# A hybrid attention block with expert lookup: the first weight unit ahead of the modulation, low-part matmuls last, transpositions and sums of the attention placed later

## The chip, the cores and the metric

The kernel runs on one core of a Trainium2 chip. The metric is device time in microseconds (us) of one execution; the median of three runs before the change is 993.6 us (992.26 to 994.26). A core has five engines that run their own instruction streams in order and wait for one another by semaphores: TensorE (PE in the profile; PEld is its weight load), VectorE (DVE), ScalarE (ACT), GpSimd (POOL) and SyncE (SP), which issues most of the DMAs.

## What is computed

The reference is one encoder layer for 256 tokens of width 1024, cut here to what the change touches:

```
mod = silu(c) @ ada_w + ada_b                 # shift1, scale1, gate1, shift2, scale2, gate2
h   = rmsnorm(x) * (1 + scale1) + shift1
q,k,v of two head groups = h @ w_in           # 8 heads each
o_A = 2-D neighbourhood attention             # learned relative bias
o_B = dilated sliding-window attention        # distance bias
x   = x + gate1 * (concat(rmsnorm(o_A), rmsnorm(o_B)) @ w_out)
h2  = rmsnorm(x) * (1 + scale2) + shift2
x   = x + gate2 * peer(h2)                    # top-16 of 128 keys, twice, then 16384 experts
out = rmsnorm(x)
```

## The kernel before

Every weight matrix comes in units of 128x1024 fp32 (0.5 MB). A unit is **split** (`split`, L89): ScalarE writes its rounded high part `hi` (L91), and `lo = raw - hi` is made by GpSimd for units of kind "b" and by VectorE for kind "c" (L93). Activations are split in the same way (`h1[0]`, `h1[1]` for the high and low part: tiles h1h, h1l). Each product is then three matmuls: high by high, weights' low part, activations' low part. The kinds of the first units stand in `KW`, `KV` and `KX`, the order in which they are loaded in `order`, and `SEQ` says how the first loads on SyncE's queue alternate between pairs of blocks of `ada_w` ("p", 1 MB) and weight units ("u").

**Modulation and projection.** `mod` is made on VectorE: `block_sum` (L208) multiplies a 128x1024 block of `ada_w` by silu(c) and sums it, one column of `mod` per pass; for a scale column a small `gain` follows (L211). For slice k = 0 to 7 of the width the first two columns (shift1, scale1) are summed, then `modulate` makes h1h (L274) and a copy t (L275) on ScalarE and `h1l = t - h1h` on VectorE (L276). In the loop over k (L513) `qk_slice` multiplies slice k by one weight unit into four PSUM banks `qkp` (8 columns of 128, three matmuls each, in `slices`, L367); after every second slice a `v_unit` and an `x_unit` follow. `LEADS[k]` says how many units ahead are split.

**Attention.** From L542 there are 12 steps: four `v_unit`, four `qk_unit`, four `wo_unit` (the output projection of group A). In step i, after the step's matmuls, `more_ada` sums further blocks of `ada_w` (`ADA[i]` pairs, two passes each), and then a pipeline over 8 pairs of heads goes on: d = 0 `att_scores` (scores sp on TensorE, bias and minimum mn on VectorE at L429, exponentials p on ScalarE), d = 1 `att_turn` (transpositions pTp), d = 2 `att_values` (op on TensorE, os on VectorE at L455), and after a group's last pair `att_norm` (squares scr, mean ms on ScalarE; power rs on GpSimd; scaling of os on ScalarE, L479); d = 3 `att_block` turns the normed output by transpositions (tp, L464) into `oT`, which `wo_unit` multiplies.

**Second norm and queries.** After the second output projection, `spread` makes the inverse root mean square of each token as a row over all partitions with one matmul (rps, L260) from a diagonal dg (VectorE, L258). Three query units are multiplied with the unnormed activation, then h2 is made from rps in eight pieces.

**The rest.** From about 186 us the kernel streams the units of `u` and `v` of the experts through TensorE, with the key selection on VectorE beside the first of them.

The framework moves independent instructions past one another when it writes each engine's queue, so the order on an engine is not that of the code; `tc.issue_after` holds an instruction behind another. The lines that the change names:

```python
SEQ = 'pupupuuuupuuppuuuuuppuuu'
LEADS = (1, 3, 2, 3, 2, 2, 3, 3)
KW = 'bbcbcbcb'
```

Of the kernel before, what the change touches and what calls it, by code (L numbers as in the profile page):

```python
# [45 lines left out]
SEQ = 'pupupuuuupuuppuuuuuppuuu'  # L46
# [3 lines left out]
LEADS = (1, 3, 2, 3, 2, 2, 3, 3)  # L50
# [4 lines left out]
KW = 'bbcbcbcb'  # L55
# [14 lines left out]
def body(tc, xT, cols, ada, w_in, e2, w_out, wq, sk, u, v, fg, const, dil, out):  # L70
    nc = tc.nc
    with ExitStack() as top:
# [92 lines left out]
        def rstd(m, pool):  # L165

            r = pool.tile([128, 2], F32, name="rs", bufs=2)
            rstd.ins = nc.gpsimd.tensor_tensor(r, m, half, op=OP.pow).ins
            return r
# [4 lines left out]
        with ExitStack() as pre:  # L174
# [88 lines left out]
            def mean_sq(ssq, n):  # L263
                m = PA.tile([128, 2], F32, name="ms", bufs=2)
                for T, c in enumerate(ssq):
                    nc.scalar.activation(m[:, T:T + 2 // len(ssq)], c, AF.Identity, scale=1.0 / n, bias=eps)
                return m
# [54 lines left out]
            m1 = mean_sq([ssq[:, 0:2]], D)  # L322
            with tc.issue_after(bank.ins):
                xp.append(bank(PP, "S"))
# [24 lines left out]
            def more_ada():  # L349
                if ada_left:  # L350
                    ada_unit(*ada_left.pop(0))
# [15 lines left out]
            def slices(k, ps, w):  # L367

                for c in range(w[0].shape[1] // 128):
                    o = ps[c // 2][:, c % 2 * S:(c % 2 + 1) * S]  # L370
                    for x, a in ((0, 0), (0, 1), (1, 0)):
                        nc.tensor.matmul(o, w[x][:, c * 128:(c + 1) * 128], h1[a][:, k, :], start=False,
                                         stop=k == 7 and c % 2 == 1 and x == 1)
                    yield
# [8 lines left out]
            def qk_slice(k, hl):  # L383

                for c, _ in enumerate(slices(k, qkp, hl)):
                    if c == CP[k]:
                        next_block(k + 2)
# [93 lines left out]
            def wo_unit(g, c2):  # L481
                hl = unit()
                hv = [t.rearrange("p (k c) -> p k c", k=4) for t in hl]
                for cc in range(2):
                    ps = PM.tile([128, 512], F32, tag="mm", name="ps")
                    for k in range(4):
                        mm3(ps[:, :S], hv[0][:, k, cc * 128:(cc + 1) * 128], hv[1][:, k, cc * 128:(cc + 1) * 128],
                            oT[0][:, 4 * g + k, :], oT[1][:, 4 * g + k, :], k == 0, k == 3)
                    b = 2 * c2 + cc
                    nc.vector.scalar_tensor_tensor(x_s[:, b, :], ps[:, :S], mod[:, 2, b:b + 1], x_s[:, b, :],  # L490
                                                   op0=OP.mult, op1=OP.add)
# [21 lines left out]
            for k in range(8):  # L513
                lead[0] = LEADS[k]
                with tc.issue_after(dg_ins):
                    hl = unit() if k < 7 else None
# [27 lines left out]
            steps += [lambda i=i: wo_unit(0, i) for i in range(4)]  # L544
            for i in range(len(steps)):
                if i == E2AT:
                    nc.sync.dma_start(e2s, e2.rearrange("p (h s k) -> p h s k", h=NH, s=6))
                steps[i]()
# [4 lines left out]
                for n in range(ADA[i]):  # L553
                    more_ada()
# [5 lines left out]
                for d in range(4):  # L560
# [13 lines left out]
                    if d == 3 and h == 6:  # L574
                        for b in range(4):
                            att_block(g, b)
# [30 lines left out]
            rps = spread(rstd(m, PA), PP, "S")  # L607
            rb2 = PA.tile([128, S], F32)
            nc.scalar.activation(rb2, rps, AF.Copy)
            early = []  # L610
            for i in range(NQ):
                hl = unit()
                ps = PM.tile([128, 512], F32, tag="mm", name="ps")
                mmT(ps[:, :S + 2], hl, xg)
# [410 lines left out]
```

## Time and profile before

| what | value |
|---|---|
| median of three runs | 993.6 us (992.26 to 994.26) |
| the profiled execution: its time | 992.28 us |
| its span, from first to last instruction | 990.5 us |
| mean granted TensorE clock | 0.985 |
| PE busy | 961.8 us (97%) |
| DVE busy | 721.0 us (73%) |
| ACT busy | 545.5 us (55%) |
| POOL busy | 446.3 us (45%) |

Around the span lie 1.8 us of the profiled execution's time. Busy shares are means over stages with different limits: the same engine can wait in one stage and set the pace in the next. A granted clock of 1.00 is TensorE's upper level (2.4 GHz), 0.50 its lower one (1.2 GHz), and a value between them is a stretch that has both.

### The profile page before, as it was taken

The numbers are of one execution on the slowest core, as the hardware profiler recorded it, in microseconds if no ns is written. First come the engines' busy times: TensorE is split into PE (matmuls) and PEld (weight loads), VectorE is DVE, ScalarE is ACT, GpSimd is POOL, SyncE is SP. The second block draws the span as 40 slices with busy tenths as digits, with TensorE's granted clock in tenths as the row PEclk, the third lists the DMA queues.
The fourth block names the chain that finished last, engine by engine and source line by source line (L and its number), as shares of the span: only waits on it lengthen the run. The fifth ranks groups of instructions, "written<-read, shape, count | busy, mean of one in ns | idle before, by whom it ended". The sixth has DMA issues, their size and how long they took to land.

```text
span 990.5 us, 17375 instructions
## 1 busy us (share of the span) xinstructions
PE 961.8 (97%) x6325; PEld 876.6 (89%) x6325; DVE 721.0 (73%) x1679; ACT 545.5 (55%) x1009; POOL 446.3 (45%) x200
## 2 busy tenths in 40 slices
PE   7899998999999999999999999999999999999996
PEld 4897887999999999999999999888888888888885
DVE  6958877799993677788888887677555555555555
ACT  3465666645444666666666565545555545445553
POOL 3677546677888677777777776000000000000002
PEclk8998999999999999999999999999999999999998
DMA  9777675355654455555554555688666566666672
GB/s 349 267 266 269 221 272 193 128 177 165 186 178 148 151 170 156 167 167 164 158 171 157 163 171 154 211 280 313 224 196 194 192 192 193 193 192 193 196 216 72
DMA packets 53397, 193.75 MB, mean 196 GB/s; under 512 B 5816, under 2 KB 6080, under 8 KB 53184
## 3 DMA queue, kind: packets, MB, share of 16 engines
q1 hardware_dynamic: 52672, 191.59, 59.3%
q8 instruction: 49, 0.80, 0.3%
q10 hardware_dynamic: 576, 1.05, 0.3%
q14 instruction: 36, 0.29, 0.1%
q0 software_dynamic: 64, 0.01, 0.0%
HBM read 190.52 MB, written 2.11 MB: 194 GB/s over the span
## 4 chain that ended last, share of the span: by engine, by line
PE 81%; DVE 1%; POOL 1%; ACT 1%; issue 1%; POOLq 0%; ACTq 0%
PE ps L130 14%; PE ps L131 14%; PE ps L132 14%; PE y L130 12%; PE y L131 12%; PE y L132 12%; PE gp L828 3%; PE scp L683 1%; DVE xgxd L586 0%; POOL GA L940 0%; DVE x_s L490 0%; POOL GA L946 0%; ACT xge2s L585 0%; ACT xsq L233 0%; PE tp L464 0%
## 5 line engine op out<-in xcount | busy, mean ns | idle before, releaser
L93 POOL TENSOR_TENSOR lo<-raw,hi 128x1024 fp32r<-128x1024 f32 x171 | 417.9, 2447 | 169.1 <-ACT hi L91 81.4
L91 ACT ACTIVATE hi<-raw 128x1024 fp32r<-128x1024 f32 x304 | 320.0, 1055 | 159.1 <-issue 61.7
L130 PE MATMUL ps<-h2h,hi 128*128 128x256 f32 x1128 | 320.5, 285 | 0.6 <-ACT GB L847 0.6
L131 PE MATMUL ps<-h2l,hi 128*128 128x256 f32 x1128 | 319.2, 283 | 0.0
L132 PE MATMUL ps<-h2h,lo 128*128 128x256 f32 x1128 | 319.0, 283 | 0.0
L93 DVE TENSOR_TENSOR lo<-raw,hi 128x1024 fp32r<-128x1024 f32 x133 | 163.3, 1228 | 135.5 <-issue 114.0
L130 PEld LDWEIGHTS ps<-h2h,hi 128*128 128x128 f32 x1128 | 216.3, 192 | 1.3 <-ACT GB L847 1.0
L131 PEld LDWEIGHTS ps<-h2l,hi 128*128 128x128 f32 x1128 | 216.5, 192 | 0.0
L132 PEld LDWEIGHTS ps<-h2h,lo 128*128 128x128 f32 x1128 | 216.3, 192 | 0.0
L130 PE MATMUL y<-hi,wx 128*128 128x512 f32 x512 | 199.3, 390 | 0.0
L132 PE MATMUL y<-hi,wx 128*128 128x512 f32 x512 | 199.3, 389 | 0.0
L131 PE MATMUL y<-lo,wx 128*128 128x512 f32 x512 | 199.3, 389 | 0.0
L896 POOL DMA_DIRECT2D g2d<-g2r x1 | 0.6, 594 | 317.0 <-ACT g2r L895 317.0
L814 DVE SCALAR_TENSOR_TENSOR gi<-iotaG,iT,gT 128x256 fp32r<-128x256 f32 x256 | 113.8, 476 | 31.5 <-PE gp L828 31.5
L130 PEld LDWEIGHTS y<-hi,wx 128*128 128x128 f32 x512 | 96.2, 188 | 20.2 <-ACT wx L866 0.2
L132 PEld LDWEIGHTS y<-hi,wx 128*128 128x128 f32 x512 | 96.1, 188 | 20.2 <-DVE wx L867 0.2
L131 PEld LDWEIGHTS y<-lo,wx 128*128 128x128 f32 x512 | 96.2, 188 | 19.5
L866 ACT ACTIVATE wx<-GB 128x256 fp32r<-128x256 f32 x90 | 37.7, 419 | 119.2 <-PE y L132 119.2
L831 DVE TENSOR_TENSOR gp<-gp,gl 128x512 f32<-128x512 f32 x64 | 44.6, 697 | 8.5 <-ACT gl L830 7.1
L811 DVE TENSOR_TENSOR jm<-iotaG,jT 128x512 fp32r<-128x512 f32 x64 | 43.6, 681 | 1.6 <-ACT iotaG L800 1.6
L208 DVE CUSTOM_DVE_ANT_0 araw<-araw,silb,col 128x1024 f32<-128x1024 f32 x24 | 41.9, 1759 | 1.1 <-DMA araw<-in_ada 1.1
L834 ACT ACTIVATE GB<-gp 128x368 f32<-128x368 f32 (+31 forms) x64 | 21.3, 332 | 37.6 <-DVE gp L831 37.6
(217 smaller groups left out, 1221.3 us busy)
## 6 DMA issues: line engine op xcount, KB each, us to landing
raw<-in_u SPq DMA_DIRECT2D x128, 512.0 KB, 3.6
raw<-in_v SPq DMA_DIRECT2D x128, 512.0 KB, 3.6
araw<-in_ada SPq DMA_DIRECT2D x20, 1024.0 KB, 7.6
raw<-in_w_in SPq DMA_DIRECT2D x24, 512.0 KB, 6.2
raw<-in_wq SPq DMA_DIRECT2D x16, 512.0 KB, 3.7
raw<-in_w_out SPq DMA_DIRECT2D x8, 512.0 KB, 8.0
GA<-in_ada SPq DMA_DIRECT2D x8, 512.0 KB, 5.2
e2s<-in_e SPq DMA_DIRECT2D x1, 1536.0 KB, 8.8
```

Source lines behind the costliest of these rows:

```text
L91: nc.scalar.activation(hi, raw, AF.Copy)
L93: ins = eng.tensor_tensor(lo, raw, hi.bitcast(F32), op=OP.subtract)
L130: nc.tensor.matmul(ps, wh, ah, start=first, stop=False)
L131: nc.tensor.matmul(ps, wh, al, start=False, stop=False)
L132: return nc.tensor.matmul(ps, wl, ah, start=False, stop=last)
L208: block_sum.ins = nc.vector.tensor_tensor_reduce(raw, raw, silb, 1.0, init, OP.mult, OP.add, m).ins
L811: nc.vector.tensor_tensor(jm, iotaG[:, None, :].to_broadcast([128, 4, 128]), jT[:, t0:t0 + 4, None].to_broadcast([128, 4, 128]), op=OP.is_ ...
L814: nc.vector.scalar_tensor_tensor(gi[:, t, :, :], iotaG[:, None, :].to_broadcast([128, 2, 128]), iT[:, t0 + t:t0 + t + 1], gT.bitcast(F32)[ ...
L828: nc.tensor.matmul(gp[:, t, :, :], jm[:, t, :], gi[:, t, :, :], start=True, stop=True)
L831: nc.vector.tensor_tensor(gp[:, :, 0, :], gp[:, :, 0, :], gl, op=OP.add)
L834: nc.scalar.activation(GB[:, m:, t0:t0 + 4], gv[:, done:, :], AF.Copy)
L866: nc.scalar.activation(wh, w, AF.Copy)
```

## The change

Four things are edited. (1) `SEQ` begins with a weight unit, so the first unit's DMA stands ahead of the first pair of `ada_w` blocks; its kind becomes "c" (VectorE makes its low part); its split is issued after the mean of squares, ahead of the diagonal; and `LEADS[0]` is 0, so that the second unit is no longer split in the same go. (2) `slices` multiplies both weight parts by h1h for all eight columns first and the weights' high part by h1l for all eight last. (3) In the attention `more_ada` stands behind the heads' pipeline of its step; group A's transpositions stand at the start of step 7 and group B's inside step 11, between the two halves of its `wo_unit`. (4) `spread` of the second norm is issued behind the first query unit.

```diff
-SEQ = 'pupupuuuupuuppuuuuuppuuu'
+SEQ = 'uppupuuuupuuppuuuuuppuuu'
-LEADS = (1, 3, 2, 3, 2, 2, 3, 3)
+LEADS = (0, 3, 2, 3, 2, 2, 3, 3)
-KW = 'bbcbcbcb'
+KW = 'cbcbcbcb'
...
             def slices(k, ps, w):
-                for c in range(w[0].shape[1] // 128):
-                    o = ps[c // 2][:, c % 2 * S:(c % 2 + 1) * S]
-                    for x, a in ((0, 0), (0, 1), (1, 0)):
-                        nc.tensor.matmul(o, w[x][:, c * 128:(c + 1) * 128], h1[a][:, k, :], start=False,
-                                         stop=k == 7 and c % 2 == 1 and x == 1)
-                    yield
+                for part in (((0, 0), (1, 0)), ((0, 1),)):
+                    for c in range(w[0].shape[1] // 128):
+                        o = ps[c // 2][:, c % 2 * S:(c % 2 + 1) * S]
+                        for x, a in part:
+                            nc.tensor.matmul(o, w[x][:, c * 128:(c + 1) * 128], h1[a][:, k, :], start=False,
+                                             stop=k == 7 and c % 2 == 1 and a == 1)
+                        if not part[0][1]:
+                            yield c
...
-            def wo_unit(g, c2):
+            def wo_unit(g, c2, between=None):
                 hl = unit()
                 hv = [t.rearrange("p (k c) -> p k c", k=4) for t in hl]
                 for cc in range(2):
+                    if cc and between:
+                        between()
...
-                with tc.issue_after(dg_ins):
+                with tc.issue_after(dg_ins if k else ms_ins):
                     hl = unit() if k < 7 else None
...
-            steps += [lambda i=i: wo_unit(0, i) for i in range(4)]
+            steps += [lambda i=i: wo_unit(0, i, att_blocks if i == 3 else None) for i in range(4)]
+
+            def att_blocks():
+                for b in range(4):
+                    att_block(1, b)
...
+                if i == 7:
+                    for b in range(4):
+                        att_block(0, b)
                 steps[i]()
...
-                for n in range(ADA[i]):
-                    more_ada()
...
-                for d in range(4):
+                for d in range(3):
...
-                    if d == 3 and h == 6:
-                        for b in range(4):
-                            att_block(g, b)
+                for n in range(ADA[i]):
+                    more_ada()
...
-            rps = spread(rstd(m, PA), PP, "S")
-            rb2 = PA.tile([128, S], F32)
-            nc.scalar.activation(rb2, rps, AF.Copy)
+            rs2 = rstd(m, PA)
...
-                mmT(ps[:, :S + 2], hl, xg)
+                ins = mmT(ps[:, :S + 2], hl, xg).ins
+                if i == 0:
+                    with tc.issue_after(ins):
+                        rps = spread(rs2, PP, "S")
+                    rb2 = PA.tile([128, S], F32)
+                    nc.scalar.activation(rb2, rps, AF.Copy)
```

How the edits move instructions is seen at three places. The first is VectorE's queue at the start of the program, before the change (sq is the square of x, araw a block of `ada_w`, xr the scaled x):

```order
L310 TENSOR_TENSOR sq_93<-sq_93 128x512
L208 ISA araw,mod<-araw,silb,col 128x1024
L208 ISA mod 128x1
L208 ISA araw,mod<-araw,silb 128x1024
L208 ISA mod 128x1
L211 TENSOR_SCALAR gain_107<-mod,gain_105,col 128x1
L338 TENSOR_TENSOR xr_170<-x_s,rps 128x256
L208 ISA araw,mod<-araw,silb,col 128x1024
L208 ISA mod 128x1
L276 TENSOR_TENSOR h1l<-t_186,h1h 128x256
```

The same place after it:

```order
L310 TENSOR_TENSOR sq_93<-sq_93 128x512
L93 TENSOR_TENSOR lo<-raw,hi 128x1024
L208 ISA araw,mod<-araw,silb,col 128x1024
L208 ISA mod 128x1
L208 ISA araw,mod<-araw,silb 128x1024
L208 ISA mod 128x1
L211 TENSOR_SCALAR gain_107<-mod,gain_105,col 128x1
L339 TENSOR_TENSOR xr_170<-x_s,rps 128x256
L208 ISA araw,mod<-araw,silb,col 128x1024
L208 ISA mod 128x1
L276 TENSOR_TENSOR h1l<-t_186,h1h 128x256
```

The first unit's low part now stands on VectorE, ahead of the first sums; the rest keeps its order.

The second is VectorE's queue in steps 1 and 2 of the attention, behind the four score passes (`st,mn<-sp`) of the first pair of heads, before the change:

```order
L208 ISA araw,mod<-araw,silb,col 128x1024
L208 ISA mod 128x1
L208 ISA araw,mod<-araw,silb,col 128x1024
L208 ISA mod 128x1
L429 ISA st,mn<-sp,e2s 128x256
L429 ISA mn 128x1
L429 ISA st,mn<-sp,e2s 128x256
L429 ISA mn 128x1
L208 ISA araw,mod<-araw,silb,col 128x1024
L208 ISA mod 128x1
L208 ISA araw,mod<-araw,silb,col 128x1024
L208 ISA mod 128x1
```

And after it:

```order
L208 ISA araw,mod<-araw,silb,col 128x1024
L208 ISA mod 128x1
L433 ISA st,mn<-sp,e2s 128x256
L433 ISA mn 128x1
L433 ISA st,mn<-sp,e2s 128x256
L433 ISA mn 128x1
L433 ISA st,mn<-sp,e2s 128x256
L433 ISA mn 128x1
L447 RECIPROCAL ri<-ri 128x2
L433 ISA st,mn<-sp,e2s 128x256
L433 ISA mn 128x1
```

Before, the second pair's last two score passes stood behind four sums; now all four stand behind one, and the other three sums follow them.

The third is ScalarE's queue at group A's norm, before the change (scr are the squares of the attention output os, ms their mean, q and pts parts of other heads):

```order
L476 ACTIVATE scr,osq<-os_901 128x512
L355 ACTIVATE q_174<-ps 128x256
L476 ACTIVATE scr,osq<-os_901 128x512
L91 ACTIVATE hi<-raw 128x1024
L266 ACTIVATE ms<-osq,eps 128x2
L597 ACTIVATE xge2s<-mod 128x8x2
L442 ACTIVATE pts<-pTp 128x512
L431 ACTIVATE p,ri<-st,mn 128x256
L479 ACTIVATE os_901<-os_901,rs 128x512 x2
```

And after it:

```order
L480 ACTIVATE scr,osq<-os_897 128x512
L356 ACTIVATE q_174<-ps 128x256
L480 ACTIVATE scr,osq<-os_897 128x512
L266 ACTIVATE ms<-osq,eps 128x2
L483 ACTIVATE os_897<-os_897,rs 128x512 x2
L91 ACTIVATE hi<-raw 128x1024
```

A unit's high part, which released a split on GpSimd ahead of the norm's power there, now stands behind the scaling of os; on GpSimd the power has moved ahead of one split.

## Rows read from the trace of the kernel before

**Rows 1.** Page: span; GB/s moved in 40 equal slices of the span.

```profile
span 990.5 us, 17375 instructions
GB/s 349 267 266 269 221 272 193 128 177 165 186 178 148 151 170 156 167 167 164 158 171 157 163 171 154 211 280 313 224 196 194 192 192 193 193 192 193 196 216 72
```

**Rows 2.** Windows: us; busy (x instructions) of PE, PEld, DVE, ACT, POOL; PEclk, DMA, GB/s.

```profile
79.91:119.44 39.53, 38.10 (x224) 30.76 (x224) 34.71 (x95) 22.54 (x59) 23.33 (x13) 0.87 0.64 232
...
119.44:151.78 32.34, 29.38 (x220) 26.76 (x219) 26.85 (x66) 19.65 (x50) 15.14 (x7) 0.95 0.70 269
...
89.66:99.66 10.00, 10.00 (x35) 8.39 (x34) 7.62 (x18) 4.44 (x11) 7.24 (x5) 0.50 0.85 310
...
130.20:133.50 3.30, 3.30 (x19) 3.30 (x18) 1.89 (x8) 3.01 (x10) 0.00 (x0) 0.54 0.60 211
...
250.00:300.00 50.00, 50.00 (x419) 50.00 (x418) 49.76 (x233) 22.99 (x36) 41.75 (x18) 1.00 0.59 181
...
186.00:975.00 789.00, 788.17 (x5223) 728.18 (x5222) 569.57 (x1394) 436.58 (x780) 328.80 (x138) 1.00 0.59 184
```

**Rows 3.** Waits of PE over the span: total us, times, longest us.

```profile
PE tp L464 <- ACT os L479: 4.5, 2, 2.3
PE qkp L372 <- DVE h1l L276: 3.9, 2, 3.7
PE qkp L372 <- ACT h1h L274: 3.1, 2, 2.8
PE sp L416 <- DVE mn L429: 1.3, 1, 1.3
...
PE rps L260 <- DVE dg L258: 0.9, 1, 0.9
```

**Rows 4.** Waits of DVE between 160 and 336 us, the longest.

```profile
DVE iT L762 <- PE rtp L756: 16.3, 1, 16.3
```

**Rows 5.** Timeline of DVE at the start: start us, us, instruction [idle before].

```profile
11.30 1.29 DVE L208 CUSTOM_DVE_ANT_0 araw<-araw,silb,col 128x1024 f32<-128x1024 f32 x1 [1.10 <-DMA araw<-in_ada]
...
13.77 0.27 DVE L211 TENSOR_SCALAR gain<-mod,gain,col 128x1 f32<-128x1 f32 x1
...
15.68 2.67 DVE L208 CUSTOM_DVE_ANT_0 araw<-araw,silb,col 128x1024 f32<-128x1024 f32 x1
...
18.28 2.55 DVE L276 TENSOR_TENSOR h1l<-t,h1h 128x256 fp32r<-128x256 f32 x1
...
22.01 0.27 DVE L211 TENSOR_SCALAR gain<-mod,gain,col 128x1 f32<-128x1 f32 x1
```

**Rows 6.** Timeline of ACT at the start.

```profile
11.53 0.26 ACT L266 ACTIVATE ms<-ssq,eps 128x2 f32<-128x2 f32 x1 [1.28 <-PE ssq L318]
13.19 0.69 ACT L256 ACTIVATE dg<-cst,rs 128x128 f32<-128x128 f32 x2 [1.40 <-POOL rs L168]
13.79 1.04 ACT L91 ACTIVATE hi<-raw 128x1024 fp32r<-128x1024 f32 x1
15.80 0.60 ACT L274 ACTIVATE h1h<-xr,mod,gain 128x256 fp32r<-128x256 f32 x1 [0.98 <-DVE xr L338]
```

**Rows 7.** Timeline of POOL: the splits of the start, and one in the attention.

```profile
14.91 2.36 POOL L93 TENSOR_TENSOR lo<-raw,hi 128x1024 fp32r<-128x1024 f32 x1 [1.04 <-ACT hi L91]
17.92 2.63 POOL L93 TENSOR_TENSOR lo<-raw,hi 128x1024 fp32r<-128x1024 f32 x1 [0.65 <-ACT hi L91]
...
126.14 2.37 POOL L93 TENSOR_TENSOR lo<-raw,hi 128x1024 fp32r<-128x1024 f32 x1 [5.07 <-ACT hi L91]
```

**Rows 8.** Timeline of ACT at group A's norm.

```profile
125.02 1.05 ACT L91 ACTIVATE hi<-raw 128x1024 fp32r<-128x1024 f32 x1
...
129.23 1.34 ACT L479 ACTIVATE os<-os,rs 128x512 f32<-128x512 f32 x2 [1.90 <-POOL rs L168]
```

**Rows 9.** Timeline of DVE in the attention, three rows.

```profile
119.36 2.80 DVE L208 CUSTOM_DVE_ANT_0 araw<-araw,silb,col 128x1024 f32<-128x1024 f32 x1
...
122.09 0.41 DVE L429 CUSTOM_DVE_ANT_0 st<-sp,dls 128x256 f32<-128x256 f32 x1
...
148.85 2.14 DVE L598 TENSOR_TENSOR xgxd<-mod,xge2s 128x16 fp32r<-128x16 f32 x1
```

More of the change, by code (lines that the diff above doesn't have):

```diff
@@ L265, in mean_sq @@
                 for T, c in enumerate(ssq):
-                    nc.scalar.activation(m[:, T:T + 2 // len(ssq)], c, AF.Identity, scale=1.0 / n, bias=eps)
+                    mean_sq.ins = nc.scalar.activation(m[:, T:T + 2 // len(ssq)], c, AF.Identity, scale=1.0 / n, bias=eps).ins
                 return m
@@ L322, in body @@
             m1 = mean_sq([ssq[:, 0:2]], D)
+            ms_ins = mean_sq.ins
             with tc.issue_after(bank.ins):
@@ L383, in qk_slice @@
             def qk_slice(k, hl):
-                for c, _ in enumerate(slices(k, qkp, hl)):
+                for c in slices(k, qkp, hl):
                     if c == CP[k]:
```

## The prediction

> **What bounds the kernel now.** I read the windows first, to find the stages in which TensorE waits. From 186 to 975 us it is busy 788.2 of 789.0 us at the full clock [rows 2]: there it is the bound, and the change leaves its work there as it is. So time can only be won or lost ahead of 186 us, and what is won there should pass through. One thing could stop it: VectorE's key selection beside the stream. But it waits 16.3 us for TensorE at its end [rows 4], so it has slack and does not hold the lead back.
>
> Then I read TensorE's waits [rows 3]. The reader is to see five: 3.7 us for the low part h1l of the first slice; 2.8 us for h1h of a later slice; 1.3 us for a score pass of VectorE; two of 2.2 to 2.3 us for the normed attention output os, one per group; 0.9 us for the diagonal of the second norm. Beside them stands the clock. After the wait of 1.3 us, among short matmuls and transpositions, TensorE ran 10.0 us at the lower level, and after the first wait for os 3.3 us at 0.54 on average [rows 2]. These cost 10.0 x 0.50 = 5.0 us and 3.3 x 0.46 = 1.5 us. All sums are made against the profiled execution's 992.3 us (its span of 990.5 us and 1.8 us around it), which lies 1.3 us under the median of 993.6; I subtract the gain from the median.
>
> **Term A, the start: gain 1.5 us.** The stall of 3.7 us has a cause in VectorE's rows: a sum that takes 1.29 us alone takes 2.67 us, and h1l, a quarter of its size, takes 2.55 us [rows 5]; at those times GpSimd made the low parts of the first two units, until 17.27 and 20.55 us [rows 7]. Both VectorE passes end 0.3 to 1.1 us after GpSimd's. So the two shut each other out. (The Trainium skill, page "SBUF — State Buffer", section "Who interferes with whom", says that a VectorE instruction with two inputs in SBUF and a GpSimd instruction that reads SBUF exclude each other, and that the one that starts first goes on undisturbed. The trace agrees with that here.)
>
> Now the first unit's high part can start behind the mean at 11.8 us and ends at 12.8 us (1.04 us), before the diagonal at 13.2 us needs ScalarE [rows 6]. Its low part takes VectorE about 1.2 us (as a sum alone, which is a pass of the same size), until 14.1 us. The first pair of sums, which ran from 11.30 to 14.04 us with its gain [rows 5], comes behind it: 14.1 + 2.7 = 16.8 us. That its block now lands half a MB later, 1.5 us at the 349 GB/s of the first slice [rows 1], is hidden: 12.8 us is before 14.1. Scaling x (0.4) and h1h (0.6) follow: the first real matmul starts at about 17.9 us instead of 16.4 us, 1.4 us later. Against that, 16 matmuls now need no low part: 16 x 0.12 = 1.9 us (50.0 us hold 419 of this size [rows 2]), until 19.8 us, while the next sum, alone, and h1l end at 17.2 + 1.3 + 0.4 = 18.9 us. The 3.7 us stall is gone. VectorE's next gain ends at 18.9 + 1.2 + 0.3 = 20.4 us where it ended at 22.28 us [rows 5], a lead of 1.9 us. But GpSimd's split of the second unit comes later (h1h and its copy go ahead of it on ScalarE): 19.4 to 22.0 us instead of 17.92 to 20.55 us [rows 7], and the next sum meets it. The chain of sums, splits and h1 that follows paces TensorE through the next slices, so its lead counts, not the stall: between 1.4 and 1.9 us, taken as 1.5. The bounds: -1.4 us if the chain is not faster and the first matmul is merely later, +3.7 us if the whole stall is won. The 2.8 us wait stays, since it is for h1h, not h1l. The new order of matmuls adds none.
>
> **Term B, the first pairs of heads: gain 3.6 us.** The score pass for which TensorE waited 1.3 us stood behind four sums; now it stands behind one. Without the wait the 10 us at the lower clock should not begin, so TensorE could win 1.3 + 5.0 = 6.3 us. VectorE allows less: from its first score pass at 79.91 us to group A's last os at 119.44 us it is busy 34.7 of 39.5 us [rows 2], 4.8 us idle, and in the new order one more sum (1.2 us) comes ahead of that os, as a count of the queue shows. 4.8 - 1.2 = 3.6 us. The bounds: 1.3 us if only the wait goes, 6.3 us.
>
> **Term C, group A's norm: gain 3.4 us.** From the score pass that ends at 122.5 us [rows 9], ScalarE, GpSimd and ScalarE again need until 130.6 us for os [rows 8], 8.1 us. In this a unit's high part (0.95 us until the next starts) stood ahead of the mean, and GpSimd's split of 2.37 us ahead of the power [rows 7]; both now stand behind. That takes up to 3.4 us from the chain, leaving 4.7. TensorE's own work between is 5.3 us before (122.5 to 127.8) and four matmuls less now, 4.8, so little or nothing of the 2.2 us is left; I count 1.9. With the wait the lower clock goes: 1.5 us. Bounds: 0 to 3.7 us. The postponed split is late for nobody: it belongs to a later step.
>
> **Term D, group B's norm: gain 2.2 us.** The second wait for os, 2.3 us, is covered from two sides: 12 matmuls (1.4 us) go ahead of the transpositions, and a small pass that sat 2.14 us on VectorE ahead of os [rows 9] now stands behind it. 1.4 + 2.1 exceeds 2.3; I leave 0.1. Bounds: 1.4 to 3.0 us, the upper one if a neighbouring wait for a PSUM bank goes too. For VectorE C and D need 5.6 us; its idle time there is 32.3 - 26.9 = 5.5 us [rows 2], so they fit, barely.
>
> **Term E, the second norm: gain 0.4 us.** Five more matmuls (0.6 us) go ahead of rps, out of a wait of 0.9 us. The h2 pieces start no earlier, as they hang on the diagonal, and TensorE meets them soon after; so 0.4. Bounds: 0 and 0.9 us.
>
> The sum is 1.5 + 3.6 + 3.4 + 2.2 + 0.4 = 11.1 us: 993.6 - 11.1 = **982.5 us**.
>
> **Rivals.**
> *VectorE paces the attention.* Terms B to D bring VectorE to its limit, and which passes meet a split of GpSimd is new. A meeting costs 1.4 to 1.5 us (2.67 or 2.80 against 1.29 [rows 5, 9]). Four more of them take 6 us from B to D: 988.5 us. For it: 34.7 busy of 39.5. Against: sums and splits are no more than before, and one split has left GpSimd. (By the skill's rule above, a meeting costs only the one that comes second; the time of this rival holds for meetings in which that is VectorE.)
>
> *The lower clock stays.* The waits shrink, but short matmuls and transpositions still stand in a row, TensorE falls to 0.50 where it did, and 5.0 and 1.5 us stay: at most the waits go, 1.5 + 1.3 + 1.9 + 2.2 + 0.4 = 7.3 us: 986.3 us. For it: the fall came after only 1.3 us of waiting. Against: the later attention steps, with the same short matmuls and no wait, ran at the full clock.
>
> *The lead is given back.* What is won by 150 us is lost before 186 us, where VectorE, ScalarE and GpSimd make the second norm: no change, 993 us. For it: the last sums now fall just there. Against: they are few (two passes, 2.4 us), and VectorE is idle there.
>
> *Slower: the lower clock through the attention.* If TensorE, now paced by VectorE in small waits between short matmuls, ran at the lower level for more than the 10 us that it does now, each 1 us of work costs 1 us more. Three steps of about 7 us, 21 us of work, at the lower level cost 21 us, less A, C, D and E (7.5 us, and B's 5.0 not won): 993.6 + 21 - 7.5 = 1007 us. It decides from 7.5 us of such work on. For it: the stretch at 89.66 us. Against: as above, later steps held the clock.
>
> **How the numbers follow.** The sum has 0.52 and, from 979.5 to 985.5 us, a range of its own; VectorE's pace 0.20; the lower clock that stays 0.12; given back 0.09; slower 0.07. The first three are faster by more than 0.2% (about 2 us, which is what a measurement of this kernel can tell): 0.84; given back is the same: 0.09; slower: 0.07. The range that holds 8 in 10 reaches from 978.5 us (A whole and B at 5 us instead of 3.6) up to 991.0 us, past VectorE's pace with two meetings more.
>
> **What would show it.** A: the wait for h1l gone, first matmul of slice 0 near 17.9 us, the gain of slice 1 near 20.4 us. B: no wait of sp for mn near 87 us, full clock from 86 to 100 us. C and D: waits of tp for os under 0.5 us each, full clock behind the first. E: wait for dg under 0.4 us. The stream begins 11 us earlier and lasts as long. It would be wrong if VectorE shows no idle time from 80 to 140 us and TensorE waits for score passes instead, if the clock row shows 0.50 in the attention for 10 us or more, or if TensorE's waits between 155 and 186 us grow by what was won.

## The result, and the profile after

The changed kernel takes 982.05 us (median of four runs, 981.32 to 984.14) beside 993.93 us for the kernel before in the same comparison (992.26 to 999.27): a ratio of 0.9875, with a 95% interval of 0.9834 to 0.9915. Its profiled execution took 981.43 us, with a span of 979.5 us, 11.0 us less than that of before [rows 1].

TensorE's waits ahead of the stream, in the changed kernel:

```profile
PE qkp L375 <- ACT h1h L274: 4.8, 3, 2.7
PE sp L420 <- DVE mn L433: 2.6, 2, 2.1
PE xp L245 <- DVE x_s L496: 1.6, 1, 1.6
PE tp L468 <- ACT pts L446: 1.3, 1, 1.3
...
PE tp L468 <- DVE oTl L472: 0.3, 1, 0.3
```

Against [rows 3], the waits for h1l, for os and for dg are gone. Those for h1h have grown, from 3.1 us in two waits to 4.8 in three, as the first matmul now comes later. New are 1.3 us at the first transposition, now for pts of another pair of heads, and a score pass that comes 2.1 us late.

The next views are windows. I cut the time ahead of the stream at four points that every kernel here has: the end of the projection's slices, the end of the fifth pair's output matmuls, the end of the eighth pair's, and the start of the query scores. First the kernel before, then the changed one, with the stream last. The counts show that the stages hold the same work: 306, 153 and 251 instructions on TensorE.

```profile
74.04:126.45 52.41, 50.98 (x306) 41.34 (x305) 46.76 (x115) 30.81 (x84) 31.14 (x17) 0.90 0.68 251
126.45:149.21 22.76, 20.56 (x153) 18.96 (x153) 17.34 (x45) 14.48 (x33) 11.45 (x6) 0.93 0.70 266
149.21:186.24 37.03, 31.40 (x251) 29.80 (x250) 26.71 (x46) 23.87 (x49) 25.25 (x15) 1.00 0.51 167
```

```profile
71.82:119.92 48.10, 45.51 (x306) 37.84 (x306) 46.49 (x114) 31.14 (x85) 34.55 (x17) 1.00 0.71 269
119.92:140.68 20.76, 18.64 (x153) 17.21 (x153) 16.74 (x45) 14.76 (x35) 10.61 (x5) 1.00 0.78 298
140.68:175.28 34.60, 31.47 (x251) 29.91 (x250) 27.39 (x48) 23.49 (x49) 26.35 (x15) 1.00 0.56 182
...
175.28:964.00 788.72, 787.79 (x5220) 727.55 (x5219) 568.53 (x1394) 436.40 (x780) 328.72 (x138) 1.00 0.59 185
```

The lead is 2.2 us at the end of the slices (74.04 to 71.82). The first five pairs add 4.3 us (52.41 to 48.10), the last three with group A's transpositions 2.0, the rest 2.4: together 10.9 us, which the stream keeps. These four numbers hang on one execution of the kernel before: against its second profile, below, they are 1.7, 6.6, 3.0 and 2.4 us. In the first stage the clock rose from 0.90 to 1.00, and VectorE is now busy 46.49 of 48.10 us.

VectorE at the start, and GpSimd's first splits:

```profile
12.68 1.22 DVE L93 TENSOR_TENSOR lo<-raw,hi 128x1024 fp32r<-128x1024 f32 x1 [2.38 <-ACT hi L91]
...
16.80 1.28 DVE L208 CUSTOM_DVE_ANT_0 araw<-araw,silb,col 128x1024 f32<-128x1024 f32 x1
...
18.05 0.42 DVE L276 TENSOR_TENSOR h1l<-t,h1h 128x256 fp32r<-128x256 f32 x1
...
19.66 0.27 DVE L211 TENSOR_SCALAR gain<-mod,gain,col 128x1 f32<-128x1 f32 x1
```

```profile
19.05 2.79 POOL L93 TENSOR_TENSOR lo<-raw,hi 128x1024 fp32r<-128x1024 f32 x1 [5.85 <-ACT hi L91]
```

The sum at 16.80 us and h1l meet no split and take 1.28 and 0.42 us, where they took 2.67 and 2.55 [rows 5].

### The profile page after: what moved, and what is told of

The parts are those of the page before. It is cut to its first block, busy times and chain, and to the rows that moved or that the text cites. A ratio compares the mean times of both kernels' runs of the same rounds, so it can differ in the third digit from the quotient of the medians.

```text
span 979.5 us, 17372 instructions
## 1 busy us (share of the span) xinstructions
PE 954.1 (97%) x6325; PEld 869.5 (89%) x6325; DVE 717.4 (73%) x1680; ACT 544.8 (56%) x1009; POOL 447.5 (46%) x199
## 4 chain that ended last, share of the span: by engine, by line
PE 82%; DVE 3%; issue 2%; POOL 1%; ACT 1%; DMA 0%; POOLq 0%; ACTq 0%; DVEq 0%
PE ps L130 14%; PE ps L131 14%; PE ps L132 14%; PE y L130 12%; PE y L132 12%; PE y L131 12%; PE gp L842 3%; DVE araw L208 1%; PE scp L697 1%; POOL lo L93 1%; PE op L457 1%; DMA raw<-in_u 0%; DVE x_s L496 0%; ACT hi L91 0%; DVE xgxd L597 0%
## 5 line engine op out<-in xcount | busy, mean ns | idle before, releaser
L130 PEld LDWEIGHTS y<-hi,wx 128*128 128x128 f32 x512 | 96.1, 188 | 20.1 <-ACT wx L880 0.2
```

The source lines that it names most:

```text
L130: nc.tensor.matmul(ps, wh, ah, start=first, stop=False)
```

## The experiments

Each experiment was timed 6 to 12 times beside the kernel before, before_again once. The changed kernel's row repeats the result above, and the time in the first row is the median beside it (the profiled execution took 992.28 us). The table gives the median, the ratio to before with its interval, the end of the slices, and the length of the three stages, all read from each run's trace at the four points named above.

| run | us | ratio (95%) | slices end | stage 1 | stage 2 | stage 3 |
|---|---|---|---|---|---|---|
| before, first profile | 993.9 | 1 | 74.0 | 52.4 | 22.8 | 37.0 |
| before, second profile | 994.9 | | 73.5 | 54.7 | 23.8 | 37.0 |
| start_unit | 993.2 | 0.9992 (0.9976 to 1.0008) | 71.7 | 50.8 | 23.8 | 38.4 |
| start_order | 988.0 | 0.9942 (0.9921 to 0.9963) | 73.6 | 47.9 | 20.5 | 40.3 |
| start_both | 986.0 | 0.9922 (0.9892 to 0.9951) | 71.5 | 47.9 | 20.0 | 40.2 |
| att_sums | 995.3 | 1.0015 (0.9997 to 1.0033) | 73.8 | 54.4 | 23.8 | 37.0 |
| all_but_order | 992.7 | 0.9982 (0.9966 to 0.9998) | 71.6 | 54.4 | 23.7 | 36.6 |
| all_but_unit | 984.0 | 0.9899 (0.9873 to 0.9924) | 73.8 | 48.8 | 20.1 | 34.6 |
| unit_on_gpsimd | 983.4 | 0.9892 (0.9868 to 0.9916) | 72.5 | 48.8 | 20.1 | 34.6 |
| the changed kernel | 982.1 | 0.9875 (0.9834 to 0.9915) | 71.8 | 48.1 | 20.8 | 34.6 |
| hold_before | 997.6 | 1.0027 (1.0015 to 1.0039) | 73.5 | 47.2 | 27.8 | 43.2 |
| hold_all_but_order | 994.2 | 0.9993 (0.9979 to 1.0008) | 72.0 | 47.3 | 27.8 | 42.8 |
| hold_all | 992.0 | 0.9972 (0.9958 to 0.9986) | 71.8 | 46.5 | 24.7 | 42.5 |
| hold_norm | 985.9 | 0.9914 (0.9891 to 0.9937) | 72.1 | 46.5 | 18.5 | 42.5 |

### The start's edits, together and apart

start_both is the kernel before with part (1) and part (2) of the change; start_unit has part (1) alone, start_order part (2) alone:

```diff
-                    for x, a in ((0, 0), (0, 1), (1, 0)):
+                for part in (((0, 0), (1, 0)), ((0, 1),)):
```

> The kernel before with the two edits of the start alone (the first unit's load, kind and split; the order of the matmuls in the slices). My theory (VectorE's chain of sums at the start sets the pace, and it has come free of the meetings with GpSimd): first matmul of slice 0 near 17.6 us, wait for h1l gone, projection's last slice 2.2 us earlier than before (near 71.8 us), and the whole lead kept: 2.2 us, about 991.5 us beside a before of 993.7. Rival (the attention of the kernel before, full of sums, takes the lead back): the slices end 2.2 us earlier, but the score wait in step 2 grows by as much and the time stays within 1 us of before.

> The kernel before with the edit of the first unit alone; the slices keep their order of matmuls. Theory (the chain of sums counts, not the order of the matmuls): h1l ends near 18.5 us, TensorE stalls for it only 0.5 to 0.9 us right behind its first matmul, slice 3 still starts near 38.0 us, and the lead at the end of the slices is 2.0 to 2.2 us. Rival (the reordered matmuls hide what is left of the stall): a stall of 1 us or more for h1l, and a lead of 1 us or less.

> The kernel before with the order of the matmuls in the slices alone. Theory: 16 matmuls (1.9 us) go ahead of the stall, so the wait for h1l shrinks from 3.7 to about 2.0 us, but the gain of slice 1 still ends near 22.3 us and the wait for h1h of slice 3 stays or grows: slice 3 starts at 40.1 us as before and the time stays within 0.5 us of before. Rival (the stall itself costs the time): slice 3 starts 1.5 to 1.9 us earlier, and so does all behind it.

At the end of the slices all three came out as the theory has it: part (1) brings 2 us there, part (2) nothing (73.6 and 71.5 us beside 73.5 to 74.0 and 71.7). But the order of the matmuls alone, which was to change nothing, made the kernel 5.8 us faster (0.58% of 994.7, by the ratio), all of it behind the slices: stage 1 fell from 52.4 or 54.7 to 47.9 us, stage 2 by 2 to 3 us. Neither theory nor rival had this. The matmuls are the same; what moved is where the framework puts instructions in the attention, on several engines. VectorE's second pair of score passes still stands behind four sums in this run. But TensorE has other work ahead of the score matmuls that wait for it. Its timeline in the kernel before, then in start_order:

```profile
86.95 0.44 PE L440 MATMUL pTp<-cst,p 128*128 128x128 f32 x2
88.72 1.35 PE L416 MATMUL sp<-k,q 64*128 64x256 f32 x6 [1.33 <-DVE mn L429]
```

```profile
86.57 0.66 PE L442 MATMUL pTp<-cst,p 128*128 128x128 f32 x4
87.06 1.00 PE L455 MATMUL op<-v,pts 128*128 128x64 f32 x8
88.31 1.13 PE L418 MATMUL sp<-k,q 64*128 64x256 f32 x6 [0.24 <-DVE mn L431]
...
94.90 1.82 PE L418 MATMUL sp<-k,q 64*128 64x256 f32 x8 [1.22 <-DVE mn L431]
```

Before, two transposition instructions stood there ahead of a wait of 1.3 us; here four of them and the first head's output matmuls (op) fill it, and 0.2 us is left. A wait of 1.2 us comes one step later, and the clock holds through the stage:

```profile
73.57:121.43 47.86, 45.81 (x306) 37.51 (x306) 44.28 (x114) 31.20 (x85) 33.88 (x17) 1.00 0.77 283
```

Stage 3 gives 3.2 us of it back (40.3 beside 37.0), half of it to a new stretch at the lower clock.

At group A's norm, too, the order alone puts the power ahead of the split. GpSimd, then ScalarE:

```profile
119.09 1.53 POOL L168 TENSOR_TENSOR rs<-ms,half 128x2 f32<-128x2 f32 x1 [5.61 <-ACT ms L266]
120.60 2.35 POOL L93 TENSOR_TENSOR lo<-raw,hi 128x1024 fp32r<-128x1024 f32 x1
```

```profile
120.66 1.34 ACT L481 ACTIVATE os<-os,rs 128x512 f32<-128x512 f32 x2 [0.69 <-POOL rs L168]
```

ScalarE stands idle for 0.7 us ahead of the scaling of os, where it stood 1.9 us before [rows 8].

### The sums alone

att_sums is the kernel before with `more_ada` behind the heads' pipeline, the first half of part (3):

```diff
-                for n in range(ADA[i]):
-                    more_ada()
                 if i < NH // 2:
...
                             att_block(g, b)
+                for n in range(ADA[i]):
+                    more_ada()
```

> The kernel before with the sums placed behind the heads' pipeline of their step, and nothing else; group B's transpositions stay where they were. Theory: the 1.3 us wait in step 2 goes and with it the 10 us at the lower clock (lead 6.8 us behind step 3's v_unit), VectorE then takes 2 to 2.5 us back in waits of the scores, group A's norm gives 2 us and keeps the clock, and group B's wait for os falls by the small pass that no longer stands ahead of it, from 2.3 us to about 0.3: in all 7.5 to 8.5 us, about 985.8 us. Rival (the clock stays down without the lead of the start, or falls elsewhere): a stretch of 10 us at 0.50 remains somewhere between 80 and 140 us, gain 3 us or less. Second rival (group B's part comes from the place of the transpositions): the wait for os stays at 2.3 us and the gain is about 5.7 us.

Gain: none. The ratio is 1.0015; this is the run in which the prediction's account of B and C fell. VectorE in this run, then its windows:

```profile
94.77 2.96 DVE L208 CUSTOM_DVE_ANT_0 araw<-araw,silb,col 128x1024 f32<-128x1024 f32 x1
...
97.66 1.73 DVE L556 TENSOR_TENSOR e2s<-cst,e2s 128x768 f32<-128x768 f32 x1
99.32 0.41 DVE L429 CUSTOM_DVE_ANT_0 st<-sp,e2s 128x256 f32<-128x256 f32 x1
```

```profile
98.50:109.50 11.00, 9.71 (x44) 8.88 (x45) 7.54 (x24) 4.71 (x13) 4.16 (x3) 0.53 0.56 197
```

Of the second pair only the last score pass still stands behind three sums (the first three behind two), and TensorE waits 0.5 us there. But two more sums and a mask of the bias (e2s) stand ahead of the third pair's last score pass. TensorE waits 3.6 us for it instead of 1.3, and the clock is down for the 10 us behind it as before, only later, as the first rival had it. At group A's norm nothing changed places either:

```profile
127.97 2.38 POOL L93 TENSOR_TENSOR lo<-raw,hi 128x1024 fp32r<-128x1024 f32 x1 [6.67 <-ACT hi L91]
130.31 1.71 POOL L168 TENSOR_TENSOR rs<-ms,half 128x2 f32<-128x2 f32 x1
```

A split still stands ahead of the power, and the wait for os is 3.2 us. Group B's wait for os stays at 2.3 us, the second rival's sign.

### Before again, and one part left out

before_again is the kernel before, profiled a second time; all_but_order and all_but_unit are the changed kernel without part (2) and without part (1); unit_on_gpsimd is the changed kernel with

```diff
-KW = 'cbcbcbcb'
+KW = 'bbcbcbcb'
```

> The kernel before, unchanged, profiled a second time: are its stretches at the lower clock a property of its order of work? Five stretches stood in the first profile (21.0, 41.5, 89.5 to 100, 130.0, and one near 11 us), 11.9 us of TensorE's work lost in all. Theory (the waits and the short matmuls of the order bring them): the same five places within 2 us, the one near 90 us again about 10 us long, span 989 to 992 us. Rival (they fall differently from execution to execution): other places or lengths, the loss differs by 3.4 us or more, and the span follows it.

> The changed kernel without the order of the matmuls in the slices (first unit, sums, transpositions and spread as changed). Theory (with the sums placed later the attention comes out in a good order only together with the slices' new order, since that alone changes what stands where in the queues): VectorE's queue in the attention is that of the sums' edit alone, the long wait of a score pass near 95 us (3.6 us there) comes again with its stretch at the lower clock, and of the lead only the start's 1.5 to 2.2 us and about 2 us of transpositions and spread stand against the 2.8 us lost: between 992 and 994 us. Rival (the edits add up: what the order brings alone, 4 to 6.5 us, is all that is missing): 986 to 988.5 us.

> The changed kernel without the edit of the first unit (its load, kind, split and the lead). VectorE's queue in the attention is that of the changed kernel. Theory (the first unit brings the start's lead of 2.2 us and nothing in the attention): no wait of 2.5 us or more for the scores, last projection matmul near 73.6 us, and 984 to 985.5 us. Rival (it also decides the attention, or the lead of the start is lost in it): within 0.8 us of the changed kernel's 982.

> The changed kernel with the first unit's low part on GpSimd instead of VectorE. Theory (a sum of VectorE and a split of GpSimd shut each other out): the split stands at 12.8 to 15.2 us, the first sum meets it and takes 2.5 to 2.8 us instead of 1.3, which is about what VectorE saves by not making the low part (1.2 us); first matmul within 0.5 us of 17.6 us, time within 1 us of the changed kernel. Rival (no exclusion, the low part is merely one pass less on VectorE): the sums take 1.3 us, first matmul near 16.3 us, and the projection ends 1.2 us earlier than in the changed kernel.

In the second profile of before the stretches fall elsewhere, as the rival has it. Its windows are

```profile
88.00:92.00 4.00, 3.84 (x17) 3.03 (x18) 3.99 (x10) 0.88 (x4) 4.00 (x3) 0.57 1.02 416
...
108.50:116.00 7.50, 7.50 (x37) 7.08 (x36) 4.90 (x20) 4.92 (x14) 3.31 (x2) 0.54 0.82 297
```

Where the first profile had 10 us in one piece from 89.66 us [rows 2], this one has 4 us there and 7 us twenty later. The stage lost as much to the clock, about 5 us (4.00 x 0.43 + 7.50 x 0.46), but no longer behind the one wait of 1.3 us. The rest of the rival did not come: the span does not follow the loss to the clock, it is 2.6 us longer at a slightly higher mean clock (0.988 beside 0.985). What grew are TensorE's waits in the attention, for score passes from 1.3 to 2.9 us, for os from 4.5 to 5.5 [rows 3]. The first of them:

```profile
PE sp L416 <- DVE mn L429: 2.9, 3, 1.4
```

all_but_order came out as the theory has it, at 992.7 us: VectorE's queue is that of att_sums, the wait of 3.6 us at the third pair is there again, and stages 1 and 2 are those of before. So is the wait for os at group B's norm, 2.3 us (5.5 less 3.2), although group B's transpositions stand where the change puts them:

```profile
PE tp L465 <- ACT os L480: 5.5, 2, 3.2
```

The edits don't add up: with part (2) the rest is worth 4 us on top of start_both, without it next to nothing beyond the start. all_but_unit, 984.0 us, shows part (1) worth about the start's 2 us and nothing in the attention. It has a stretch at 0.57 that the changed kernel lacks, yet its stage 1 is only 0.7 us longer, as it is in unit_on_gpsimd, which has such a stretch too. Most of the 1.7 us lost there (4.00 x 0.43) cost nothing, with VectorE busy throughout the stretch:

```profile
103.50:107.50 4.00, 3.96 (x18) 3.13 (x19) 4.00 (x14) 3.25 (x7) 1.59 (x1) 0.57 0.59 192
```

With the first unit on GpSimd, VectorE and GpSimd meet:

```profile
13.52 3.36 DVE L208 CUSTOM_DVE_ANT_0 araw<-araw,silb 128x1024 f32<-128x1024 f32 x1
```

```profile
13.26 2.54 POOL L93 TENSOR_TENSOR lo<-raw,hi 128x1024 fp32r<-128x1024 f32 x1
```

The split began first, took its usual time and ended at 15.80 us; the sum ended 1.1 us later, after 3.36 us instead of 1.22. That is 2.1 us lost for 1.2 saved; the slices end 0.7 us later than in the changed kernel and the first matmul comes 0.6 us later. The theory holds, at a price above the one expected (3.4 us against 2.5 to 2.8), and the first matmul and the time, 1.3 us above the changed kernel's, just miss what was forecast of them. (By the Trainium skill, page "SBUF — State Buffer", section "Who interferes with whom", the one that starts first goes on and the other blocks until it has ended. The two rows agree.)

### The sums held by hand

If VectorE's queue is what decides, the four score passes of a pair should stay together. For hold_before I expected by this that the wait of 3.6 us goes, that at most one stretch at the lower clock is left between 80 and 145 us, and 985.5 to 988 us. hold_before is att_sums with each step's sums held behind the last score pass of the step; hold_all_but_order and hold_all have the same hold in all_but_order and in the changed kernel:

```diff
                 for n in range(ADA[i]):
-                    more_ada()
+                    with tc.issue_after(att_scores.ins):
+                        more_ada()
```

> The kernel before with the sums behind the heads' pipeline, as in the run of the sums alone, and each step's sums now held in VectorE's queue behind that step's last score pass. All four score passes of a pair then stand together, and the queue of the attention no longer depends on the order of the matmuls in the slices. [...] Rival (the slices' order acts by itself, on TensorE): no better than the sums alone, 993 to 996 us.

> The changed kernel without the order of the matmuls in the slices, and with the sums held behind the score passes. Its queues in the attention are those of the next run. Theory: with the queue fixed by hand the slices' order is worth nothing more than what it hides at the start (0 to 1 us): within 1.5 us of the next run and 8 us or more ahead of the run without the hold (992.6). Rival (the order of the matmuls is itself what counts): 990 us or more.

> The changed kernel with the sums held behind the score passes. Theory (the 2.1 us wait of the scores near 101 us comes from two sums that stand between a pair's score passes and meet a split): that wait falls under 0.5 us and 1 to 2 us are won, 980 to 981.5 us. Rival (VectorE is busy throughout from 80 to 120 us, so the wait only moves, to the output passes os or to group A's norm): 981.5 to 984 us, the same as the changed kernel.

For stage 1 the theory holds, in all three: 46.5 to 47.3 us, also without any edit of the start, with waits for score passes of 0.6 us or less in all and no stretch at the lower clock. The hold also moves work, though: 12 of the sums fall into stage 1 instead of 16, so part of this may be the sums that have left it. And the times I had expected were missed by 9 to 12 us: stages 2 and 3 lost more than stage 1 won, hold_before and hold_all_but_order came out at their rivals' times or above, and hold_before, at 1.0027, is slower than before. TensorE's waits in hold_all, and GpSimd at its group A's norm:

```profile
PE tp L467 <- ACT pts L445: 2.6, 1, 2.6
PE tp L467 <- ACT os L482: 1.8, 1, 1.8
```

```profile
116.75 2.59 POOL L93 TENSOR_TENSOR lo<-raw,hi 128x1024 fp32r<-128x1024 f32 x1 [1.93 <-ACT hi L91]
119.31 0.72 POOL L168 TENSOR_TENSOR rs<-ms,half 128x2 f32<-128x2 f32 x1
```

The hold moved a split ahead of the power again, at both norms, and ScalarE stood 3.2 us at the scaling of os with the next pair's exponentials and pts behind it. The 2.6 us wait for pts is that. Behind it the clock fell for 7 us:

```profile
125.50:132.50 7.00, 7.00 (x26) 4.32 (x25) 2.75 (x10) 2.95 (x6) 2.35 (x1) 0.51 0.86 294
```

hold_all is 2.2 us faster than hold_all_but_order, more than the 1.5 us expected, and stage 2 has the difference (24.7 beside 27.8). In both a sum of VectorE stands ahead of three score passes shortly before group A's norm, and GpSimd starts two splits beside it. First hold_all_but_order, then hold_all:

```profile
109.43 3.45 DVE L208 CUSTOM_DVE_ANT_0 araw<-araw,silb,col 128x1024 f32<-128x1024 f32 x1
...
109.43 5.70 POOL L93 TENSOR_TENSOR lo<-raw,hi 128x1024 fp32r<-128x1024 f32 x2 [1.02 <-ACT hi L91]
```

```profile
108.94 1.27 DVE L208 CUSTOM_DVE_ANT_0 araw<-araw,silb,col 128x1024 f32<-128x1024 f32 x1
...
109.22 5.60 POOL L93 TENSOR_TENSOR lo<-raw,hi 128x1024 fp32r<-128x1024 f32 x2 [1.30 <-ACT hi L91]
```

In the one the sum starts with the split and takes 3.45 us; the score passes behind it and the norm's mean come 2.7 us later than in hold_all, TensorE waits 4.1 us for pts, and the clock is down for 10 us instead of 7. In the other the sum starts 0.3 us ahead of the split and takes 1.27 us. hold_before has the meeting of the first (3.38 us) and its wait of 4.1. This is read from three traces; no run varies the meeting alone.

### The norm's chain freed

If the held sums lost their time at the norms, because a high part stands ahead of the mean and one split more ahead of the power, then with these held back the waits of 2.6 and 1.8 us should fall under 1.3 and 0.5 us. By this I expected most of the time at the lower clock behind them to go, and 981 to 986 us. hold_norm is hold_all with one unit's split at each norm held behind the mean on ScalarE and behind the power on GpSimd (i counts the units):

```diff
+                with ExitStack() as held:
+                    for ins in behind if i in (25, 29) else ():
+                        held.enter_context(tc.issue_after(ins))
-                ready.append(split(i, loaded.pop(0) if loaded else load(i), eng))
+                    ready.append(split(i, loaded.pop(0) if loaded else load(i), eng))
...
                 rn = rstd(mean_sq([sq], 512), PA)
+                behind[:] = mean_sq.ins, rstd.ins
```

> The run before (the changed kernel with its sums held behind the score passes), and with one unit's split held behind the mean on ScalarE and behind the power on GpSimd, at each of the two groups' norms; GpSimd's queue then has as many splits ahead of group A's power as in the changed kernel, two fewer than in the run before. [...] Rival (the transpositions are late for another reason, VectorE's passes os or the place of the transpositions): the waits stay within 0.5 us and the time within 2 us of 992.

Both waits at the transpositions are gone, and so is the stretch behind the first. GpSimd at group A's norm, and TensorE from 112 to 140 us:

```profile
116.35 0.72 POOL L172 TENSOR_TENSOR rs<-ms,half 128x2 f32<-128x2 f32 x1 [3.68 <-ACT ms L270]
```

```profile
112.00:140.00 28.00, 27.98 (x231) 26.22 (x230) 23.38 (x65) 19.91 (x53) 11.83 (x6) 1.00 0.85 306
```

Stage 2 took 18.5 us instead of 24.7, and the kernel won 6 us (992.0 to 985.9). Up to the last output matmul it is the fastest of all, 3.6 us ahead of the changed kernel (137.1 beside 140.7 us). It loses that and more in stage 3, which is as long as in hold_all. Its one long wait there is now for the output projection's update x_s, and a stretch at the lower clock is left beside it:

```profile
PE ps L134 <- DVE x_s L500: 6.9, 4, 5.1
```

```profile
146.20:153.00 6.80, 3.96 (x18) 3.94 (x19) 6.30 (x14) 0.95 (x2) 4.15 (x2) 0.50 0.53 170
```

VectorE ahead of x_s:

```profile
142.67 2.18 DVE L212 CUSTOM_DVE_ANT_0 araw<-araw,silb 128x1024 f32<-128x1024 f32 x1 [1.79 <-DMA araw<-in_ada]
...
144.78 3.35 DVE L212 CUSTOM_DVE_ANT_0 araw<-araw,silb 128x1024 f32<-128x1024 f32 x1
...
148.43 0.47 DVE L500 SCALAR_TENSOR_TENSOR x_s<-ps,mod,x_s 128x256 f32<-128x256 f32 x1
```

The stretch costs about 2 us (3.96 us of work at 0.50). Ahead of x_s stand two postponed sums. The first waits 1.8 us for its block of `ada_w`; both take 1.0 to 2.1 us more than the 1.2 us that such a sum takes alone, beside three splits that GpSimd makes in a row. No kernel here beats the changed one.

## Why the prediction was right, and where it was not

The time, the sign and the sum came out, and the changes of the stages lie near the terms; what the prediction read as the cause of the two largest terms did not hold. That the time came so near is in part luck. The edits to which B and C were put down, added to start_both, change stages 1 and 2 by +0.2 and +0.8 us. What brings both terms is the order of the slices' matmuls, which was put at nothing (start_order: 47.9 and 20.5 us); it takes 3.2 us back in stage 3, and there the rest of the change wins 5.6.

**Term A, 1.5 us; measured 2.2.** Right, and a little small (1.7 against the second profile): the first matmul came at 17.57 us (17.9 predicted), the gain of slice 1 ended at 19.93 (20.4), the stall for h1l is gone. The lead was counted at the low end of 1.4 to 1.9 us. start_unit shows that the unit's edit alone does it. unit_on_gpsimd brings back one meeting with GpSimd and loses 0.7 us of the lead; what of the rest is the unit's earlier load and split and what the second unit's later split was not run apart.

**Term B, 3.6 us; measured 4.3 in stage 1.** The size was right (6.6 against the second profile), and so was its bound: VectorE, busy 46.49 of 48.10 us, now paces the stage, and the wait of 2.1 us is the first rival's, at a price that left the term standing. In the stretch for which the term was worked out, from the first score pass to group A's last os, 39.5 us have become 36.0:

```profile
77.76:113.73 35.97, 33.42 (x230) 27.71 (x229) 35.49 (x93) 22.30 (x59) 27.08 (x13) 1.00 0.61 227
```

That is the 3.6 us of the term, but not by its working. The trace counts 13 sums in this stretch before and 12 after, one fewer and not one more; VectorE's idle time went into meetings, five sums of over 1.9 us where there were three. The sign of being wrong that names VectorE without idle time and TensorE waiting for score passes came in part, from 80 to 120 us (VectorE busy 39.5 of 40 us), without the loss. The full clock from 86 to 100 us came too.

The step that failed is the sentence under term A, "The new order of matmuls adds none". True of the start, it was taken for the whole program. In the attention the new order of the slices' matmuls goes along with other queues, TensorE's and VectorE's: without it (all_but_order) stage 1 stays at 54.4 us with the wait and the lower clock, with nothing else (start_order) it is 47.9. I had read the changed queue of VectorE from the whole change and put it down to the place of the sums, which by itself gives a third queue, no better than the first. hold_before agrees with the mechanism behind the term, that a score pass kept waiting behind sums costs the stage: with the score passes kept together, stage 1 takes 47.2 us with none of the start's edits. It doesn't prove it, since four sums have left that stage as well. start_order shows a second way to the same end, other work of TensorE in the place of the wait. That a late score pass must bring the lower clock is not shown: start_order waits 1.2 us for one a step later, the changed kernel 2.1 us, and both keep 1.00.

**Term C, 3.4 us; measured 2.0 in stage 2.** The chain was read rightly. In the changed kernel mean, power and scaling of os follow one another with no high part or split between:

```profile
118.14 0.30 ACT L266 ACTIVATE ms<-osq,eps 128x2 f32<-128x2 f32 x1
119.27 1.34 ACT L483 ACTIVATE os<-os,rs 128x512 f32<-128x512 f32 x2 [0.83 <-POOL rs L168]
```

```profile
118.52 0.72 POOL L168 TENSOR_TENSOR rs<-ms,half 128x2 f32<-128x2 f32 x1 [3.97 <-ACT ms L266]
```

And hold_norm shows that this order is worth 6 us where it is missing. The term was too large because TensorE's wait at the first transposition did not fall to 0.3 but to 1.3 us: it is for pts, which has to leave a PSUM bank and stands behind the scaling of os and a high part on ScalarE. Another 0.8 us, for oTl, is new. Here too the cause is the order of the slices: with it alone (start_order) the power is ahead of the split and stage 2 takes 20.5 us, with the sums alone (att_sums) neither.

**Terms D and E, 2.2 and 0.4 us, less what is given back; measured 2.4 in stage 3.** The wait for os of 2.3 us is gone (0.3 us are left at that place, for oTl), and so is the one for dg, and TensorE's wait at xp grew from 1.0 to 1.6 us. The place of the transpositions alone does not cover the wait for os: in all_but_order, which has it, 2.3 us are left, in start_both, which has the order without it, 1.1 us. Beyond that these parts were not run one by one. Beside start_both they are, with the sums, worth 5.6 us in this stage (40.2 to 34.6), more than D and E, since the order of the slices alone loses 3.2 us there; beside start_unit, so without the order, they are worth 1.8 us (38.4 to 36.6). Which of the three does how much stays open.

**The rivals.** The lower clock that stays is what all_but_order shows, and the lead given back what start_order and hold_norm show in stage 3; in the changed kernel neither came. Slower than before was hold_before, by the chain of the norm and the postponed sums; the clock fell with them, to 0.82 in stage 2 and 0.88 in stage 3, but not in stage 1.

Some of the prediction's sums are off by little: 17.9 less 16.4 us is 1.5, not 1.4; C and D need 5.6 us, which is more than the 5.5 us that VectorE is idle; and what stands beside the ends of the wide range gives 978.9 and about 991.4 us, not 978.5 and 991.0.

## What to carry to other kernels

Where a framework orders the queues, a queue that differs between two versions belongs to all edits together: build each edit alone and compare the queues of every engine, far from the edit too, before a term is put down to one of them. A short chain across engines (here mean, power and scaling) is worth guarding against the long passes that may slip in ahead of it, and so is a group of small passes that frees a buffer. Work that fills gaps must still be done: postponed far enough, it meets the next chain, and the transfer that feeds it becomes late as well.

## What the runs showed of the hardware

The same program had its stretches at the lower clock elsewhere in a second execution: 10 us in one piece against 4 and 7 us apart, with spans of 990.5 and 993.1 us. Over the 86 executions of it beside the experiments the mean clock lies between 0.978 and 0.991; those at 0.991 took 989 to 991 us, those at 0.979 and below 998 to 999. One profile shows how much TensorE loses to the clock in such a stage (5 us in both), but not that it loses it behind a certain wait. And where VectorE paces a stage, a stretch at 0.57 that took 1.7 us of TensorE's work went with a stage only 0.7 us longer (all_but_unit).

Of a sum of VectorE and a split of GpSimd that begin within 0.3 us of each other, the order decides: the sum took 1.27 us when it began 0.3 us ahead, and 3.36 to 3.45 us when it began with the split or 0.3 us behind it (hold_all, unit_on_gpsimd, hold_all_but_order).
